# The output product of a decoder layer as one seven-product run on 512-column quarters, with loads six ahead

## The chip, the cores and the metric

The kernel runs on one core of one Trainium2 chip. The core has a matrix engine (TensorE, PE in the profile), a vector engine (VectorE, DVE), a scalar engine (ScalarE, ACT), a general engine (GpSimd, POOL) and a queue that only issues transfers (SyncE, SP). The metric is the device time of one launch in microseconds (us). The kernel before takes 770.54 us, the median of three runs (770.27 to 772.26).

## The reference

One decoder layer over 512 tokens of width 1024 in float32:

```
h = rms_norm(x, norm_mix);  proj = h @ w_in
y_pool = pool_mixer(u, w_pool);  y_nsa = nsa_mixer(q, ...)          # 16 heads, 2 groups
merged = g_a * (y_pool @ w_proj_pool) + g_b * (y_nsa @ w_proj_nsa)
x = x + merged @ w_out                                              # 512x1024 @ 1024x1024
h = rms_norm(x, norm_mlp)
x = x + square(relu(h @ w_ff1)) @ w_ff2                             # width 4096
out = rms_norm(x, norm_final)
```

`merged @ w_out` is the product that is rebuilt.

## The kernel before, in words

**Products in two halves of precision.** Each float32 operand is held as a high part H (a reduced format that PE takes at full rate) and a low part L, the rest. A product is three matmuls: H by H, H by L, L by H. A weight tile is loaded from memory (`raw`), ACT copies it to `wh` or `w3h` (the high part), and DVE subtracts to get `wl` or `w3l`. Weights that only pass through lie in three ring slots of such pairs; others have resident slots (`W1H`, `W1L` here).

**Seven products instead of eight.** A big product is cut into 2x2 blocks and computed with seven block products (Strassen's scheme in Winograd's form), named by the weight side: A11, A12, A22 are weight blocks, S1 to S4 are sums of them. The activation side has its own sums, T1 to T4. The sums of weights are not computed by an engine: SP copies one block to memory (`S<-w_ff`, `S_o<-w_out`) and POOL issues a transfer that adds the other block to it; the sum is then loaded like a weight.

**Order.** Python generators emit the instructions; each engine works through its own list in order. `pieces` and `Wide.pe` emit matmuls and, between them, call `ahead()` (which prepares the next weight) and `step_side()` (which lets each waiting side job emit its next instruction). `emit_load` issues a load when a `raw` buffer is free (there are `RAW` = 4); the table in `sums_after` says behind which load the next weight sum is begun. So a change of a product's shape moves the instructions of all engines.

**The stages around the change.** After attention come eight products pn0 to pn7 with `w_proj_nsa`, 24 matmuls of 512 columns each, which give the merged activation, 128 features at a time (`GB`, split to `mH`, `mL`). Two of the four tiles for the direct half of `w_out` are prepared between them. Then:

- columns 0 to 511 of `merged @ w_out` by seven products on quarters of 256 tokens and 256 columns (class `Out`, L1647): 168 matmuls of 256 columns, from seven weight tiles, three of which are sums made in memory and one (S4) is made by DVE from S2 and A12;
- columns 512 to 1023 directly, token tile by token tile (`tm3_resident`, L568): 96 matmuls of 512 columns from four resident tiles; after each token tile `post1` starts `to_fm(t)`.

`to_fm` is the chain that opens the MLP: add the product to x (`add_x`), sum of squares on ACT, square root, reciprocal, scale by the norm (`xs`, DVE), transposes on PE in fours (L1841), then high and low parts of the transposed activation (`R`) and the sums T1 to T4. The first products of the MLP, A11 and A12 of both column groups (`FIRST[0]`, L638), are interleaved with the chains of the last tokens; S1 of the MLP comes next and needs T1.

Of the kernel before, what the change touches and what calls it, by code (L numbers as in the profile page):

```python
# [13 lines left out]
F32 = mybir.dt.float32  # L14
FR = mybir.dt.float32r
# [47 lines left out]
def trunk(ctx: ExitStack, tc: tile.TileContext, A, out):  # L63
# [38 lines left out]
    WL, LD = [], []  # L102
    RAW = 4

# [79 lines left out]
    for j in range(8):  # L184
        add_cols(f"pn{j}", w_pn, 128 * j)
        if j in (5, 6):
            add_rows(f"wo1{j - 5}", w_o, 256 * (j - 5), 512)
    WO_LATE = {"A22": 2, "S4": 3}
    WO_TURN = ("A11", "S1", "S3", "S2", "A12", "A22", "S4")
    wo_at = {}  # L190
    late, later = [], []
    wo_of = {f"A{i + 1}{j + 1}": w_o[512 * j:512 * j + 512, 256 * i:256 * i + 256].rearrange("(k p) c -> p k c", p=128)
             for i in range(2) for j in range(2)}
    for o, x, y in (("S1", "A21", "A22"), ("S3", "A11", "A21"), ("S2", "S1", "A11")):
        wo_of[o] = dp.tile([128, 4, 256], F32, name=f"{o}_o")
        jobs.append((wo_of[o], wo_of[x], wo_of[y]))
    for o in WO_TURN:
        if o in wo_of:
            wo_at[o] = len(LD)
            LD.append([(wo_of[o], 0)])  # L200
        WL.append((f"{o}2o0", None))
        if o in WO_LATE:
            add_rows(f"wo1{WO_LATE[o]}", w_o, 256 * WO_LATE[o], 512)
    MLP0 = len(LD)
# [15 lines left out]
    def add_group(layer, c, g):  # L220

        q = quarters(layer, c, g)
        of = {"A" + k: v for k, v in q.items()}
        final = layer == 2 and c == LAST
        for o in ("S1", "S3", "S2", "S4")[:LASTSUMS if final else 4 - layer]:
            of[o] = dp.tile(list(q["11"].shape), F32, name=f"{o}_{layer}{c}{g}")
        jobs.append((of["S1"], q["21"], q["22"]))
        jobs.append((of["S3"], q["11"], q["21"]))
        if late:
            jobs.append(late.pop())  # L230
# [40 lines left out]
    raws, hls = {}, {}  # L271
    st = {"load": 0, "prep": 0, "use": 0, "kept": 0, "pairs": 0, "sums": 0}
    spare, slots_hl = [], []
# [74 lines left out]
    def shifted(tiles, key):  # L348

        o = 56 if key[-2] == "G" or key in ("ck", "ks") else 8 if key[:2] in ("wk", "wv") else 16 if key[-2] == "o" else 0  # L350
        return [t[:, o:o + 1024] for t in tiles]

    def slot_of(i):

        return shifted(slot_tiles(i), WL[i][0])
# [105 lines left out]
    def wo_steps(i):  # L461

        o = WL[i][0][:-3]
        if o in wo_at:
            while st["load"] <= wo_at[o]:
                assert emit_load()
            kept[o] = raws.pop(wo_at[o])[0]
        h, l = slot_of(i)
        t = kept.pop("A12" if o == "S4" else o)
        with behind(held_back[0]) if held_back and o == "S2" else nullcontext():  # L470
            ACT.activation(h, t, AF.Copy)
        yield
        with behind(held_back[1]) if held_back and o == "S2" else nullcontext():
            DVE.tensor_tensor(l, t, h.bitcast(F32), op=ALU.subtract)
        hls[i] = tuple(x.rearrange("p (a b) -> p a b", a=4) for x in (h, l))
        if o == "A12":
            yield
            DVE.tensor_tensor(t, t, kept["S2"], op=ALU.add)
        if o in ("A12", "S2"):
            kept[o] = t  # L480
            if o == "S2":
                return
            kept.pop("S2")
# [1091 lines left out]

    def tm3_resident(ws, aT, post):

        for t in range(NT):
            ps = bank()
            prods = []  # L1580
            for k in range(8):
                wH, wL = ws[k // 2]
                prods += split_products(*aT(k, t), wH[:, k % 2, :], wL[:, k % 2, :])
            for _ in pieces(ps, prods, prepare=t > 0):
                step_side()
            post(t, ps)

    def keep(keys, tiles):
# [12 lines left out]
    junk = [None]  # L1601

    def add_x(t, h, ps):
        DVE.tensor_tensor(X1[t][:, 512 * h:512 * h + 512], ps, X1[t][:, 512 * h:512 * h + 512], op=ALU.add)

# [124 lines left out]
    with ExitStack() as c3:  # L1730
        q3 = c3.enter_context(pool("q3"))
        gB = q3.tile([128, D], F32, name="gB1")
        nc.sync.dma_start(gB, bcast(A["norm_mlp"][0], D))
        q3.tile([128, 56], F32, name="gap")
        mT = (q3.tile([128, 8, S], FR, name="mH"), q3.tile([128, 8, S], FR, name="mL"))
        W1 = (q3.tile([128, 8, S], FR, name="W1H"), q3.tile([128, 8, S], FR, name="W1L"))
        junk[0] = q3.tile([128, 512], F32, name="junk")
        keep([f"wo1{i}" for i in range(4)], W1)

        def mTs(k, t):  # L1740
            return [m[:, k, 128 * t:128 * t + 128] for m in mT]

# [5 lines left out]
        for j in range(3):  # L1748
            split_m(j)
        w1 = []  # L1750

        class Merged:
# [42 lines left out]
        for j in range(3, 8):  # L1795
# [3 lines left out]
            fm3(f"pn{j}", post, OT)  # L1799
            if j in (5, 6):  # L1800
                w1.append(use(f"wo1{j - 5}"))
            if j >= 6:
# [8 lines left out]
        side.append(M.split())  # L1811
        first = Out("o", 0, M)
        for o in WO_TURN:
            first.pe(o)
            if o in WO_LATE:
                w1.append(use(f"wo1{WO_LATE[o]}"))

        def folded0():
            while first.done != set(first.X):
                yield  # L1820
            for n, _ in enumerate(first.fold()):
                if n % 3 == 0:
                    yield
            for t in range(NT):
                square_sum(t, 0)
            summed.append(0)
        summed = []
        side.append(folded0())

        def to_fm(t):  # L1830
            xs = q3.tile([128, D], F32, tag="xs", bufs=1, name="xs")
            add_x(t, 1, PS1[t])
            square_sum(t, 1)
            normed(t, xs)
            for _ in range(5 + (t == 0)):
                yield
            th, sl = t // 2, slice(128 * (t % 2), 128 * (t % 2) + 128)
            for a in range(2):
# [8 lines left out]
                if b != "12":  # L1847
                    DVE.tensor_tensor(XB[b][1][:, :, sl], src, XB[b][0][:, :, sl].bitcast(F32), op=ALU.subtract)
                yield
            if th == 0:  # L1850
                return
            for o, d, x, y in (("T1", XT, XQ["11"], XQ["12"]), ("T3", XQ["12"], XQ["22"], XQ["12"]),
                               ("T2", XQ["11"], XQ["22"], XT)):
                DVE.tensor_tensor(d[:, :, sl], x[:, :, sl], y[:, :, sl], op=ALU.add if o == "T2" else ALU.subtract)
                ACT.activation(XB[o][0][:, :, sl], d[:, :, sl], AF.Copy)
                yield
# [14 lines left out]

        PS1 = {}

        def post1(t, ps):
            until(lambda: summed)
            PS1[t] = ps
            g = to_fm(t)
            next(g)
            side.append(g)
        tm3_resident(w1, mTs, post1)  # L1880
    a4 = ctx.enter_context(pool("a4"))
# [70 lines left out]
    for c in range(4):  # L1952
        Y = Hidden(c == LAST)
        gs = [Group(f"1{c}{g}", XB.get, bank, (pair(GBf, 6 + g), pair(MAf, 6 + g), pair(MAf, 0), pair(MAf, 1)),
                    (lambda g, Y: lambda src, f, th: Y.act(src, g, f, th))(g, Y)) for g in range(2)]
        if c == 0:
            for o in FIRST[0]:
                for g in gs:
                    g.pe(o)
            while not turned[0]:  # L1960
# [124 lines left out]
```

## Time and profile before

| | |
|---|---|
| median of the runs | 770.54 us |
| span of the profiled execution, first to last instruction | 767.4 us |
| what lies around the span, against the median | 3.1 us |
| PE, DVE, ACT, POOL busy | 756.7, 666.4, 511.1, 184.2 us |
| granted clock of PE | full in all slices |
| pn3 to pn7 | from 378.2 |
| seven-product half of the output product | 405.4 to 425.6 |
| direct half, with the transposes | 425.6 to about 449 |
| transfers: accumulates from POOL | 50, of which 9 are issued ahead of attention, 9 in it, 32 after |

The profiled execution has no time of its own beside its span; 767.4 is the number against which its rows add up, and the median is 3.1 us above it. A busy time is the union of an engine's instructions; rows of the chain of waits give start, length and the group of instructions; rows of a window give its stretch, its length and each engine's busy time with the number of instructions.

### The profile page before, as it was taken

Reading aid. Unit: us, or ns where it says so; the run is one execution under the profiler, and the core shown is the slowest. Engines: PE = TensorE matmul, PEld = TensorE weight load, DVE = VectorE, ACT = ScalarE, POOL = GpSimd, SP = SyncE. Lnnn points to the kernel's source line nnn. Section 1 sums busy time; section 2 is a strip of 40 time slices with the busy share of each in tenths; the row PEclk is TensorE's granted clock in tenths of the full one; section 3 lists DMA queues with packets and bytes.
Section 4 is the critical chain, followed back from the end, with each engine's and each line's share of the span. In section 5 each row is a group of like instructions: output and inputs, shape, how many; then the busy total and the mean of one; then the engine's idle time right before and its main releaser. Section 6 shows DMA issues by size and latency. Waiting matters only on the chain.

```text
span 767.4 us, 13409 instructions
## 1 busy us (share of the span) xinstructions
PE 756.7 (99%) x4757; PEld 675.9 (88%) x4757; DVE 666.4 (87%) x1279; ACT 511.1 (67%) x977; POOL 184.2 (24%) x264
## 2 busy tenths in 40 slices
PE   9999999999999999999999999999999999999996
PEld 7889889888888888888889899989998999889985
DVE  7897999548988889989689689997989788978897
ACT  7766655328878888898745576954774477447754
POOL 4001010117746766574000200111111110111001
PEclk9999999999999999999999999999999999999999
DMA  9559993983051833371357965989998999799942
GB/s 308 165 143 266 251 230 108 257 214 115 15 176 52 158 56 70 56 138 60 116 186 220 324 111 185 287 219 299 310 259 222 314 303 257 215 325 294 293 171 110
DMA packets 119886, 150.76 MB, mean 196 GB/s; under 512 B 5782, under 2 KB 92346, under 8 KB 119611
## 3 DMA queue, kind: packets, MB, share of 16 engines
q1 hardware_dynamic: 98250, 122.90, 48.3%
q0 software_dynamic: 21280, 26.22, 22.8%
q8 instruction: 38, 0.62, 0.3%
q10 hardware_dynamic: 288, 0.79, 0.3%
q14 instruction: 30, 0.24, 0.1%
HBM read 145.16 MB, written 54.53 MB: 260 GB/s over the span
## 4 chain that ended last, share of the span: by engine, by line
PE 84%; DVE 9%; ACT 2%; DMA 2%; issue 1%; POOL 1%; SPq 0%; DVEq 0%; ACTq 0%; POOLq 0%
PE psB L638 20%; PE psB L1698 18%; PE psF L568 16%; PE psB L568 6%; PE psV L638 5%; PE psS L1378 4%; PE psT L1440 4%; PE psO L1474 4%; PE psB L1647 3%; DMA raw<-w_in 2%; PE psF L700 1%; DVE wl L527 1%; DVE PT L1456 1%; DVE P L1400 1%; DVE wkt L527 1%
## 5 line engine op out<-in xcount | busy, mean ns | idle before, releaser
L343 POOL DMA_DIRECT2D S<-w_ff x44 | 49.0, 1113 | 351.3 <-DMA S<-w_ff 290.3
L568 PE MATMUL psF<-R,wh 128*128 128x512 f32 x384 | 124.6, 400 | 0.0
L390 ACT ACTIVATE wh<-raw 128x1024 fp32r<-128x1024 f32 x73 | 77.1, 1058 | 70.0 <-PE psB L638 24.0
L1423 POOL TENSOR_SCALAR P<-P,sm,GT 128x128 f32<-128x128 f32 (+3 forms) x128 | 85.5, 724 | 68.8 <-DVE sm L1420 36.1
L395 DVE TENSOR_TENSOR wl<-raw,wh 128x1024 fp32r<-128x1024 f32 x73 | 88.9, 1219 | 12.7 <-ACT wh L390 12.2
L568 PEld LDWEIGHTS psF<-R,wh 128*128 128x128 f32 x384 | 68.8, 188 | 11.4 <-issue 0.2
L1410 ACT ACTIVATE P<-P,sm 128x128 f32<-128x128 f32 (+3 forms) x128 | 71.0, 557 | 9.9 <-DVE sm L1400 6.2
L568 PE MATMUL psF<-R,wl 128*128 128x512 f32 x192 | 75.5, 393 | 0.0
L524 ACT ACTIVATE wh<-raw 128x512 fp32r<-128x512 f32 (+1 forms) x76 | 45.1, 616 | 32.9 <-PE psF L568 21.2
L1400 DVE CUSTOM_DVE_ANT_0 P<-psS,cst 128x128 f32<-128x128 f32 (+3 forms) x128 | 59.3, 482 | 4.9 <-PE psT L1440 2.7
L390 ACT ACTIVATE w3h<-raw 128x1024 fp32r<-128x1024 f32 x37 | 39.2, 1059 | 34.0 <-PE psB L638 12.6
L527 DVE TENSOR_TENSOR wl<-raw,wh 128x512 fp32r<-128x512 f32 (+1 forms) x74 | 51.5, 707 | 9.2 <-ACT wh L524 8.9
L1451 ACT ACTIVATE PT<-psT 128x512 fp32r<-128x512 f32 (+2 forms) x96 | 49.0, 520 | 13.9 <-PE psT L1440 13.0
L1456 DVE TENSOR_TENSOR PT<-psT,PT 128x512 fp32r<-128x512 f32 (+2 forms) x96 | 56.2, 591 | 1.5 <-ACT PT L1451 1.3
L1440 PE MATMUL psT<-ident,P 128*128 128x128 f32 x320 | 50.1, 273 | 0.6 <-POOL rx L899 0.4
L395 DVE TENSOR_TENSOR w3l<-raw,w3h 128x1024 fp32r<-128x1024 f32 x37 | 45.1, 1220 | 4.7 <-ACT w3h L390 4.5
L1474 PE MATMUL psO<-PT,VV 128*128 128x256 f32 x320 | 48.5, 286 | 0.0
L1440 PEld LDWEIGHTS psT<-ident,P 128*128 128x128 f32 x320 | 39.6, 140 | 9.4 <-POOL rx L899 0.8
L638 PE MATMUL psB<-R,wh 128*128 128x256 f32 x336 | 46.3, 279 | 0.0
L1474 PEld LDWEIGHTS psO<-PT,VV 128*128 128x128 f32 x320 | 42.2, 188 | 1.3 <-ACT PT L1451 0.3
L638 PEld LDWEIGHTS psB<-R,wh 128*128 128x128 f32 x336 | 42.5, 188 | 0.2
L568 PEld LDWEIGHTS psF<-R,wl 128*128 128x128 f32 x192 | 36.0, 188 | 7.5
(442 smaller groups left out, 2083.7 us busy)
## 6 DMA issues: line engine op xcount, KB each, us to landing
raw<-w_ff SPq DMA_DIRECT2D x54, 512.0 KB, 6.2
S<-w_ff POOLq DMA_DIRECT2D x44, 512.0 KB, 8.2
raw<-S SPq DMA_DIRECT2D x44, 512.0 KB, 5.3
S<-w_ff SPq DMA_DIRECT2D x32, 512.0 KB, 7.3
raw<-w_in SPq DMA_DIRECT2D x31, 512.0 KB, 4.7
S<-S SPq DMA_DIRECT2D x12, 512.0 KB, 6.7
raw<-w_proj_nsa SPq DMA_DIRECT2D x8, 512.0 KB, 4.1
x<-x SPq DMA_DIRECT2D x7, 512.0 KB, 6.5
```

What stands on the lines that cost most here:

```text
L390: ACT.activation(h, t, AF.Copy)
L395: DVE.tensor_tensor(l, t, h.bitcast(F32), op=ALU.subtract)
L527: eng.tensor_tensor(l[:, sl], t[:, sl], h[:, sl].bitcast(F32), op=ALU.subtract)
L568: PE.matmul(ps, a, b, start=first and j == 0, stop=last and j == n - 1, skip_group_check=True)
L638: PE.matmul(out, w[u][:, k, 128 * f:128 * f + 128], moving[v][:, k, :], **kw)
L1400: DVE.tensor_tensor_reduce(out=P[:, o:o + n].rearrange("p (a c) -> p a c", c=128), in0=s, in1=m, scale=1.0, scalar=3e38, op0=ALU.add, op1= ...
L1410: last_exp[:] = [ACT.activation(c, c, AF.Exp, bias=sm[:, 0, e:e + 1], scale=-1.0, accum_out=sm[:, 1, e:e + 1])]
L1423: r = POOL.tensor_scalar(P[:, o:o + n], P[:, o:o + n], sm[:, 2, e:e + 1], GT[:, qb, c + e:c + e + 1], op0=ALU.mult, op1=ALU.mult)
L1440: PE.transpose(pt[:, 128 * j:128 * j + 128], P[:, 128 * j:128 * j + 128], ident)
L1456: return DVE.tensor_tensor(dL, src, dH.bitcast(F32), op=ALU.subtract)
L1474: PE.matmul(ps[:, qb % 2, :, :], VV[:, k, b, g, :], t[:, j, :, :], start=False, stop=last and j == len(kbs) - 1 and t is tL, skip_group_ch ...
L1698: PE.matmul(ps[f], self.Y.of(y)[u][:, 2 * g + k, 128 * f:128 * f + 128], w[v][:, k, :], start=first and g == k == u == v == 0, stop=g == k ...
```

## The change

The whole `merged @ w_out` becomes one seven-product run with quarters of 256 tokens and 512 columns (class `Mixed`, built on `Wide`, which the MLP's second product already uses). Each weight block of 512x512 is loaded as two halves of 256 rows: 14 halves, eight of them sums made in memory (S4 too; DVE no longer adds A12 and S2). A11, S3 and S4 go to the resident slots, the rest to the ring. The order is A11, S3, S2, A12, A22, S1, S4; S4 accumulates on the PSUM banks of S1 after S1 has been added to x, and is written out token by token so that `to_fm` of tokens 2 and 3 can follow; tokens 0 and 1 are complete after A22. The direct half is gone. The MLP's first products start when tokens 0 and 1 are shaped.

Loads run six ahead: `RAW` is 6, with two loads more at the start of the program, back to four ahead in attention (`spared`), and six again near the MLP. Sums of weights are begun earlier: POOL issues 10 accumulates ahead of attention, 16 in it and 29 after, 55 in all. `xs` has two buffers. The memory of the transfer descriptors is set to 8192 bytes instead of the default.

```diff
-    RAW = 4
+    RAW = 6
...
-    WO_TURN = ("A11", "S1", "S3", "S2", "A12", "A22", "S4")
+    WO_TURN = ("A11", "S3", "S2", "A12", "A22", "S1", "S4")
...
+    for g in range(2):
+        wo_of.append({f"A{i + 1}{j + 1}": w_o[512 * j + 256 * g:512 * j + 256 * g + 256, 512 * i:512 * i + 512].rearrange(
+            "(k p) c -> p k c", p=128) for i in range(2) for j in range(2)})
+    for o, x, y in (("S3", "A11", "A21"), ("S2", "S3", "A22"), ("S1", "A21", "A22"), ("S4", "S2", "A12")):
+        for g, of in enumerate(wo_of):
+            of[o] = dp.tile([128, 2, 512], F32, name=f"{o}_o{g}")
+            (late if o == "S4" else jobs).append((of[o], of[x], of[y]))
...
+        if i == N1 and st["spared"] < 2:
+            st["spared"] += 1
+            return True
...
+        if i == MLP0 - 6:
+            for _ in range(2):
+                emit_load()
...
-            return i in EARLY or i in (26, 27, 33, 35, 36) or N1 + 3 <= i < N1 + len(FILL2) or i == MLP0 - 2
+            return (i in EARLY or i in (26, 27, 33, 35, 36) or N1 + 3 <= i < N1 + len(FILL2) + 5) + (i in (N1 + 9, N1 + 11, N1 + 13))
         if i < MLP0 + 12:
-            return {3: 1, 6: 4}.get(i - MLP0, 0)
+            return 5 * (i == MLP0 + 6)
...
+    with behind(made[0]):
+        for _ in range(2):
+            emit_load()
...
-                for o, b, n in (("T1", "11", 1), ("T2", "22", 2), ("T4", "21", 3)):
+                for o, b, n in (("T2", "22", 1), ("T4", "21", 2), ("T1", "11", 3)):
...
-            if j in (5, 6):
-                w1.append(use(f"wo1{j - 5}"))
...
+        class Mixed(Wide):
+            def pe(self, o):
+                if o != "S4":
+                    super().pe(o)
+                    return
+                until(lambda: "S1" in self.done)
+                ws = [use(f"S42o{g}") for g in range(2)]
+                ps = self.ps["d"]
+                for f in range(2):
+                    prods = []
+                    for g in range(2):
+                        for k in range(2):
+                            y = [x[:, 2 * g + k, 128 * f:128 * f + 128] for x in self.Y.of("22")]
+                            prods += split_products(*y, *(v[:, k, :] for v in ws[g]))
+                    for _ in pieces(ps[f], prods, first=False):
+                        step_side()
+                    side.append(self.end(f, ps[f]))
+            def end(self, f, ps):
+                yield
+                x = XX[:, 2 + f, 0:512]
+                DVE.tensor_tensor(x, x, ps, op=ALU.add)
+                square_sum(2 + f, 0, 1)
+                yield from to_fm(2 + f)
...
+        mixed_o = Mixed("o", M)
+        for o in WO_TURN:
+            mixed_o.pe(o)
+        until(lambda: {0, 1} <= set(shaped))
...
+        for o in FIRST[0]:
+            for g in gs0:
+                g.pe(o)
+        until(lambda: len(shaped) == 4)
...
+    nc = bacc.Bacc("TRN2", target_bir_lowering=False, num_devices=1, dynamic_dma_scratch_size=8192)
```

Three places show how this moves instructions. The first is ACT's list in the pn stage, where the weights of pn4 to pn6 are prepared. Before (`raw_4518` is pn4's weight, `raw_4725` pn5's; `W1H` gets the tiles of the direct half):

```order
L524 ACTIVATE W1H<-raw_4828 128x512 [waits DMAHW2_49]
L524 ACTIVATE W1H<-raw_4828 128x512
L524 ACTIVATE wh_4916<-raw_4518 128x512 [waits DMAHW6_49,PE_49,Activation_49]
L524 ACTIVATE wh_4916<-raw_4518 128x512
L1746 ACTIVATE mH<-GB 128x512 [waits DVE_49]
L524 ACTIVATE W1H<-raw_4928 128x512 [waits DMAHW4_49]
L524 ACTIVATE W1H<-raw_4928 128x512
L524 ACTIVATE wh_4954<-raw_4725 128x512 [waits DMAHW7_49,PE_49,Activation_49]
L524 ACTIVATE wh_4954<-raw_4725 128x512
```

And in the change (`raw_4532` is pn4's weight, `raw_4746` pn5's, `raw_4849` pn6's; `raw_4949`, `raw_4987` are the halves of A11, `raw_5024`, `raw_5062` those of S3):

```order
L474 ACTIVATE W1H<-raw_4949 128x1024 [waits DMAHW7_49]
L519 ACTIVATE wh_4937<-raw_4532 128x512 [waits DMAHW5_49,PE_49,Activation_49]
L519 ACTIVATE wh_4937<-raw_4532 128x512
L1729 ACTIVATE mH<-GB 128x512 [waits DVE_49]
L474 ACTIVATE W1H<-raw_4987 128x1024 [waits DMAHW0_49]
L474 ACTIVATE W1H<-raw_5024 128x1024 [waits DMAHW3_49]
L519 ACTIVATE wh_4975<-raw_4746 128x512 [waits PE_49,Activation_49]
L519 ACTIVATE wh_4975<-raw_4746 128x512
L1729 ACTIVATE mH<-GB 128x512 [waits DVE_49]
L474 ACTIVATE W1H<-raw_5062 128x1024 [waits DMAHW4_49]
L519 ACTIVATE wh_5012<-raw_4849 128x512 [waits PE_49,Activation_49]
L519 ACTIVATE wh_5012<-raw_4849 128x512
```

Two tiles of output weights stood ahead of pn5's in this stretch; now three do, and the weights of pn5 and pn6 themselves no longer wait for a transfer there. A12's first half (`raw_5119`) stands ahead of pn7's in the same way.

The second place is SP's list at that time in the change; `S_210` to `S_211` are copies for sums of the MLP's weights, `S_o` are the sums of `w_out`:

```order
L339 DMA S_210_98<-w_ff 256x1x512 [waits DMAHW5_49]
L339 DMA S_111_96<-S_111_94 16x8192 [waits DMAHW6_49,DMASW0_49]
L298 DMA raw_4949<-w_out 128x2x512 [waits DMAHW7_49,DVE_49]
L298 DMA raw_4987<-w_out 128x2x512 [waits DMAHW0_49,DVE_49]
L339 DMA S_211_99<-w_ff 256x1x512 [waits DMAHW1_49]
L339 DMA S_211_100<-w_ff 256x1x512 [waits DMAHW2_49]
L298 DMA raw_5024<-S_o_73 128x1024 [waits DMAHW3_49,DVE_49]
L298 DMA raw_5062<-S_o_74 128x1024 [waits DMAHW7_49,DMAHW4_49,DVE_49]
```

Before, SP issued no such copy between pn0 and the middle of the output product; now five (with `S_210_97`) stand in the pn stage, and five accumulates on POOL belong to them and their forerunners.

The third place is DVE's list around the end of the new product, from the adds of A12's result (first row) to that of S1's first half (last row); `x` is the residual, `psB` the results, `raw_5280` an MLP weight:

```order
L1701 TENSOR_TENSOR x_4904<-x_4904,psB 128x512 [waits PE_49] x2
L477 TENSOR_TENSOR wl_5171<-raw_5178,wh_5170 128x1024 [waits DMAHW0_49,Activation_49]
L1593 TENSOR_SCALAR sq<-sq 128x1 [waits Activation_49] x2
L477 TENSOR_TENSOR W1L<-raw_5242,W1H 128x1024 [waits DMAHW2_49]
L1701 TENSOR_TENSOR x_4904<-x_4904,psB 128x512 [waits DVE_49,PE_49] x2
L399 TENSOR_TENSOR wl_5150<-raw_5280,wh_5149 128x1024 [waits DMAHW4_49,DVE_49,Activation_49]
L1600 RECIPROCAL sq<-sq 128x1 [waits Activation_49]
L1701 TENSOR_TENSOR x_4904<-x_4904,psB 128x512 [waits PE_49]
```

and PE's list at the same place:

```order
L1681 MATMUL psB<-wh_5170,R_65 128x512 x4
L563 MATMUL psB<-W1H,mH 128x512 [waits DVE_49]
L563 MATMUL psB<-W1L,mH 128x512
L563 MATMUL psB<-W1H,mL 128x512
L1849 MATMUL psB<-ident,xs 128x128 [waits DVE_49]
L1849 MATMUL psB<-ident,xs 128x128 x3
L563 MATMUL psB<-W1H,mH 128x512
```

The second row is S4's first matmul; the DVE instruction it waits for is the last of the DVE rows. Before, S1 was the second of the seven, five products ahead of S4.

More of the change, by code (lines that the diff above doesn't have):

```diff
@@ L185, in trunk @@
         add_cols(f"pn{j}", w_pn, 128 * j)
-        if j in (5, 6):
-            add_rows(f"wo1{j - 5}", w_o, 256 * (j - 5), 512)
-    WO_LATE = {"A22": 2, "S4": 3}
-    WO_TURN = ("A11", "S1", "S3", "S2", "A12", "A22", "S4")
+    WO_TURN = ("A11", "S3", "S2", "A12", "A22", "S1", "S4")
     wo_at = {}
[L191 to L196, printed above, removed]
-    for o in WO_TURN:
[L198 to L203, printed above, removed]
+    late, later, wo_of = [], [], []
+    for g in range(2):
[5 more added lines that the diff above has]
+            (late if o == "S4" else jobs).append((of[o], of[x], of[y]))
+    for o in WO_TURN:
+        for g, of in enumerate(wo_of):
+            key = f"{o}2o{g}"
+            wo_at[key] = len(LD)
+            WL.append((key, len(LD)))
+            LD.append([(of[o], 0)])
     MLP0 = len(LD)
@@ L461, in wo_steps @@
     def wo_steps(i):
[L463 to L470, printed above, removed]
+        key = WL[i][0]
+        while st["load"] <= wo_at[key]:
+            assert emit_load()
+        t = raws.pop(wo_at[key])[0]
+        h, l = dest[key][:2] if key in dest else slot_of(i)
+        late_one = held_back and key == "S22o0"
+        with behind(held_back[0]) if late_one else nullcontext():
             ACT.activation(h, t, AF.Copy)
         yield
-        with behind(held_back[1]) if held_back and o == "S2" else nullcontext():
+        with behind(held_back[1]) if late_one else nullcontext():
             DVE.tensor_tensor(l, t, h.bitcast(F32), op=ALU.subtract)
[L475 to L483, printed above, removed]
+        hls[i] = tuple(x.rearrange("p (a b) -> p a b", a=2) for x in (h, l))
         if st["load"] > RAW + MLP0:
@@ L1733, in trunk @@
         nc.sync.dma_start(gB, bcast(A["norm_mlp"][0], D))
-        q3.tile([128, 56], F32, name="gap")
+        q3.tile([128, 64], F32, name="gap")
         mT = (q3.tile([128, 8, S], FR, name="mH"), q3.tile([128, 8, S], FR, name="mL"))
-        W1 = (q3.tile([128, 8, S], FR, name="W1H"), q3.tile([128, 8, S], FR, name="W1L"))
+        W1 = [q3.tile([128, 4104], FR, name=f"W1{e}") for e in "HL"]
         junk[0] = q3.tile([128, 512], F32, name="junk")
-        keep([f"wo1{i}" for i in range(4)], W1)
-        def mTs(k, t):
-            return [m[:, k, 128 * t:128 * t + 128] for m in mT]
+        for n, o in enumerate(("A11", "S3", "S4")):
+            for g in range(2):
+                m = (2 * n + g) % 4
+                dest[f"{o}2o{g}"] = [t[:, 1024 * m + 8 * (o == "S3"):][:, 0:1024] for t in W1] + [f"W1{m}"]
         ACT.activation(tick, GB[:, 7, 0:1], AF.Sqrt)
@@ L1828, in trunk, with take @@
-        side.append(folded0())
+        class Mixed(Wide):
[8 more added lines that the diff above has]
+                    prods = []
+                    for g in range(2):
+                        for k in range(2):
[5 more added lines that the diff above has]
+            def end(self, f, ps):
+                yield
+                x = XX[:, 2 + f, 0:512]
+                DVE.tensor_tensor(x, x, ps, op=ALU.add)
+                square_sum(2 + f, 0, 1)
+                yield from to_fm(2 + f)
+            def take(self, o, ps):
+                yield from super().take(o, ps)
+                if o == "S2":
+                    for i, j in ((1, 0), (1, 1), (0, 1)):
+                        for f in range(2):
+                            x = XX[:, 2 * j + f, 512 * i:512 * i + 512]
+                            DVE.tensor_tensor(x, x, self.U[:, f, :], op=ALU.subtract if i else ALU.add)
+                            yield
+                elif o == "A12":
+                    for t in range(2):
+                        square_sum(t, 0)
+                elif o == "S1":
+                    for t in range(2, 4):
+                        square_sum(t, 1, 0)
+                elif o == "A22":
+                    for t in range(2):
+                        square_sum(t, 1)
+                    for t in range(2):
+                        yield from to_fm(t)
@@ L1854, in to_fm @@
                 DVE.tensor_tensor(d[:, :, sl], x[:, :, sl], y[:, :, sl], op=ALU.add if o == "T2" else ALU.subtract)
+                while o not in XB:
+                    yield
                 ACT.activation(XB[o][0][:, :, sl], d[:, :, sl], AF.Copy)
@@ L1870, in fourth_sum, with act0, act @@
             turned[0] += 1
[L1872 to L1880, printed above, removed]
+        shaped = []
+        mixed_o = Mixed("o", M)
+        for o in WO_TURN:
+            mixed_o.pe(o)
+        until(lambda: {0, 1} <= set(shaped))
+        Y0 = []
+        def act0(g):
+            def act(src, f, th):
+                while not Y0 or not turned[0]:
+                    yield
+                yield from Y0[0].act(src, g, f, th)
+            return act
+        gs0 = [Group(f"10{g}", XB.get, bank, (pair(GBf, 6 + g), pair(MAf, 6 + g), pair(MAf, 0), pair(MAf, 1)),
+                     act0(g)) for g in range(2)]
+        for o in FIRST[0]:
+            for g in gs0:
+                g.pe(o)
+        until(lambda: len(shaped) == 4)
     a4 = ctx.enter_context(pool("a4"))
```

49 lines of the change are left out of this document (9 added, 40 removed).

## The prediction

> **What bounds the kernel now.** First the page: which engine is busy, and what the chain that ended last is made of.
>
> ```profile
> span 767.4 us, 13409 instructions
> PE 756.7 (99%) x4757; PEld 675.9 (88%) x4757; DVE 666.4 (87%) x1279; ACT 511.1 (67%) x977; POOL 184.2 (24%) x264
> PE 84%; DVE 9%; ACT 2%; DMA 2%; issue 1%; POOL 1%; SPq 0%; DVEq 0%; ACTq 0%; POOLq 0%
> ...
> q1 hardware_dynamic: 98250, 122.90, 48.3%
> q0 software_dynamic: 21280, 26.22, 22.8%
> ```
>
> TensorE (PE) has work 99% of the span, so a matmul less is time less, unless a wait fills its place; 10.7 us of the span are PE gaps, and that is all that better feeding of PE could ever win. The span is 767.4 us, 3.1 below the median of the runs (770.54); I make the sum against 767.4 and add 3.1 at the end. A change within 0.3% (2.3 us: 768.2 to 772.9) is what a measurement of this kernel cannot tell from none.
>
> Next the chain of waits around the output product, in order of time (start, length, what).
>
> ```profile
> 378.23 27.21 PE psB L568 x120
> 405.44 20.12 PE psB L1647 x168
> 425.56 13.65 PE psB L568 x60
> 439.20 0.44 PE psB L1841 x4
> 439.64 1.39 PE psB L568 x6
> ...
> 455.27 10.74 PE psB L638 x92
> ```
>
> From 378.23 on the chain is PE alone, with no gap. The 120 matmuls are pn3 to pn7 (24 each, 0.2268 us apart): they start at 378.23, 383.67, 389.11, 394.55 and 400.0. At 405.44 begins the seven-product half of the output product (168 matmuls of 256 columns, 0.1198 each), at 425.56 the direct half (60+36 of 512 columns, 0.2275 each), between whose later pieces stand the transposes of the normed tokens in fours.
>
> Third, how full the other engines are there (span of the window, its length, busy time of PE, PEld, DVE, ACT, POOL, then clock, DMA share, GB/s).
>
> ```profile
> 360.00:380.00 20.00, 20.00 (x104) 17.01 (x103) 13.27 (x26) 15.04 (x27) 1.10 (x1) 1.00 0.39 132
> 380.00:400.00 20.00, 20.00 (x90) 16.57 (x89) 16.62 (x26) 8.13 (x14) 0.00 (x0) 1.00 0.51 159
> 400.00:420.00 20.00, 20.00 (x148) 18.96 (x148) 19.63 (x25) 12.83 (x16) 1.18 (x1) 1.00 0.79 239
> 420.00:440.00 20.00, 20.00 (x113) 17.41 (x113) 14.42 (x25) 9.48 (x20) 3.36 (x3) 1.00 1.02 329
> 440.00:460.00 20.00, 20.00 (x141) 18.41 (x140) 15.40 (x25) 14.34 (x28) 2.19 (x2) 1.00 0.71 116
> ```
>
> VectorE (DVE) is nearly full from 400 to 420 and has 10 us free from 420 to 460. The clock is full throughout.
>
> **Matmuls removed.** 168×0.1198 and 96×0.2275 are 20.12+21.84 = 41.96 us; now 168 matmuls of 512 columns run, 168×0.2270 = 38.13. The same number and width take this in the MLP:
>
> ```profile
> 567.70 38.13 PE psB L1698 x168
> ```
>
> That is **−3.83 us**, if PE never waits. Transposes and the MLP's products only change places on PE.
>
> **The wait at S4.** S1 and S4 now stand next to each other and share a PSUM accumulator, so S4's first matmul waits until DVE has added S1's result to x. Whether DVE is there in time follows from its queue. The spacing of its instructions:
>
> ```profile
> 405.67 0.68 DVE L1245 TENSOR_TENSOR GB<-psB,GB 128x512 f32<-128x512 f32 x1
> ...
> 410.24 0.68 DVE L1771 TENSOR_TENSOR R<-GB,R 128x512 fp32r<-128x512 f32 x1
> 410.85 0.69 DVE L1779 TENSOR_TENSOR GB<-GB 128x512 f32<-128x512 f32 x1
> 411.45 1.22 DVE L474 TENSOR_TENSOR wl<-raw,wh 128x1024 fp32r<-128x1024 f32 x1
> 412.58 2.35 DVE L1791 TENSOR_TENSOR R<-GB,R 128x1024 fp32r<-128x1024 f32 x2
> ```
>
> A 128x512 one follows after 0.60, a 128x1024 one after 1.13. In the changed order 7 of the first and 6 of the second kind stand from pn7's PSUM read (405.67) to the first add of a product: 4.2+6.8 = 11.0, so that add starts at 416.7, although A11 is ready at 405.4+5.45 = 410.9. With the other add DVE is through at 417.9. Then the preparation of A12's second half waits for its ring slot, which S2's first half leaves at 405.4+13.6 = 419.0; ACT needs 1.06 (below), so DVE starts at 420.1. From there to A22's first add stand seven weight lows and ten adds: 7×1.13+10×0.60+0.2 = 14.1, so 434.2; A22 was ready at 432.7. Behind that add follow, each waiting for the one before:
>
> ```profile
> L390 ACT ACTIVATE wh<-raw 128x1024 fp32r<-128x1024 f32 x5 | 5.3, 1060 | 1.4 <-PE psB L1647 1.3
> L1608 ACT ACTIVATE junk<-x 128x512 f32<-128x512 f32 x8 | 5.1, 632 | 9.1 <-DVE x L1604 6.4 <-DVE x L1673 2.5
> L1608 ACT ACTIVATION_READ_ACCUMULATOR junk<-x 128x1 f32 x8 | 1.5, 186 | 0.0
> ```
>
> the add (0.68), a square on ACT (0.63+0.19), the MLP weight's high part (1.06), its low part on DVE (1.13), a reciprocal (0.15) and then S1's add (0.68): 434.2+4.4 = 438.6, and with semaphores about 438.9. PE ended S1 at 438.1. The least wait is S1's own: its first PSUM half ends 0.45 before the product, a matmul drains in about 0.4, the add takes 0.68, so 0.6 even with DVE free (0.4 where the drain is shorter). The most: each of three ring slots that DVE waits for costs it up to a whole low, +2, so 3. **+1.5** taken: 0.8 by the count, and part of one such wait.
>
> **Behind S4.** DVE has 3 weight lows' worth more in this stage than before, and x/U additions in full width, while PE has 3.8 us less; of the 10 us free above, 3.8 go with PE's time and about 5 (2 on weights, 3 on adds) into work. The token chains (reciprocal, two scalings at 0.71, transposes, halves of T) therefore queue behind weight lows: the MLP's first product waits for R's low half behind one 1.13 low, about 0.6, and the transposes of tokens 2 and 3 up to 0.4 each. **+1.0** (0 to 2). What covers these chains is no longer the direct product but the 96 MLP matmuls of 256 columns (11.4 us) of FIRST; the chain of tokens 2 and 3 needs about that, so MLP's S1 isn't the next one late.
>
> **Earlier loads in the pn stage.** ACT's queue now holds the high parts of five output weights ahead of pn4 to pn7's, so an output weight that lands late holds up pn weights. The rows before:
>
> ```profile
> 381.84 0.37 SPq L297 DMA_DIRECT2D raw<-w_proj_nsa  x1
> ...
> 382.98 1.15 ACT L524 ACTIVATE W1H<-raw 128x512 fp32r<-128x512 f32 x2 [1.11 <-DMA raw<-w_out]
> 384.04 1.14 ACT L524 ACTIVATE wh<-raw 128x512 fp32r<-128x512 f32 x2
> ```
>
> Here pn5 is prepared at 384.04, 5.1 us before PE needs it (389.11), although ACT had waited 1.11 for an output weight. In the new order S3's first half (a sum, read back) is loaded at about the same moment as that SP row, 381.4 to 381.9, when a buffer comes free, and pn5 stands behind it: 1.06 for it, 0.62 for pn5's first high half, 0.68 for the low half, 2.36 in all. It must land by 386.75, 4.9 to 5.3 us after issue. The same holds for A12's first half ahead of pn7 (issued near 391, wanted by 397.6: 6.6 us). What a load takes:
>
> ```profile
> raw<-w_out SPq DMA_DIRECT2D x6, 512.0 KB, 4.0
> ...
> raw<-w_ff SPq DMA_DIRECT2D x4, 512.0 KB, 5.9
> S<-w_ff SPq DMA_DIRECT2D x4, 512.0 KB, 7.8
> S<-w_ff POOLq DMA_DIRECT2D x6, 512.0 KB, 10.7
> ```
>
> The first is from 370 to 410, the others from 406 to 442, where the DMA share is 1.02. Which applies? q0 carries the 50 accumulates: 22.8% of 767.4 is 175 us, 3.5 each on all 16 engines; q1 moves 122.90 MB in 371 us, 1.58 per 0.52 MB. From 360 to 406 the windows hold about 7.8+10.2+5 = 23 us of transfers; the change moves five sum copies (SP) and five accumulates (POOL) into it, +25: 48 us in 46, as full as 420 to 440. So 5.9 rather than 4.0, and pn5 0.6 to 1.0 late, at 4.0 not at all. **+0.5** (0 to 2.9, the copies' 7.8).
>
> [...]
>
> **Front.** Two extra loads at the start and six buffers can at best remove what waits for loads there:
>
> ```profile
> PE psC L997 <- DVE wkt L527: 0.7, 1, 0.7
> ...
> ACT wpl L524 <- DMA raw<-w_pool: 3.2, 1, 3.2
> ```
>
> PE waits 0.7 once; ACT's 3.2 for w_pool lies ahead of it. **−0.4** (−0.9 to 0).
>
> **Attention.** Seven more accumulates are issued there, each holding POOL 1.11 us:
>
> ```profile
> L343 POOL DMA_DIRECT2D S<-w_ff x44 | 49.0, 1113 | 351.3 <-DMA S<-w_ff 290.3
> ...
> 300.00:320.00 20.00, 19.56 (x132) 17.10 (x131) 18.84 (x60) 16.94 (x47) 12.43 (x20) 1.00 0.10 27
> 320.00:340.00 20.00, 20.00 (x133) 17.89 (x133) 17.77 (x61) 16.99 (x46) 15.64 (x24) 1.00 0.70 112
> ```
>
> Behind them in POOL's queue stand the P scalings that the transposes wait for. But the window with several accumulates (15.64 busy) has PE no less busy than the one without (12.43). **0** (0 to 2: of 7.8 us the quarter that might fall into a head's chain).
>
> **Sum.** −3.83+1.5+1.0+0.5−0.4 = −1.2: span 766.2, time **769.3**. The five extra accumulates, nine more SP rows, the smaller descriptor scratch and the wider xs lie beside PE work: POOL is 24% busy.
>
> **Rivals.** (a) DVE keeps up: S1's add waits only its 0.6, the tokens cost 0.4, the loads land at 4.0 to 5: −3.83+0.6+0.4−0.4 = −3.2, time 767.3. For it: 10 us free on DVE; against: the first add is 5.8 late already. 0.33. (b) Slower: the loads in the pn stage. It decides from a landing of about 9 us: with S3's half landing like an accumulate (10.7), pn5 is 5.6 late instead of 0.5, and everything behind shifts: 769.3+5.1 = 774.4. For it: 48 us of transfers in 46, and the scarcity of slack (5.1 us); against: SP's loads landed at 5.9 in a window as full. 0.16. (c) Attention pays: a POOL issue ahead of a P scaling delays PE by half of its 1.11: 7 of them +3.9, time 773.2. For it: POOL's queue is in order; against: the two windows above. 0.06. (d) The change doesn't take effect, since the waits eat 3.8 whole and the rest is neutral: 770.5, part of the forecast's case.
>
> **Chances.** The forecast's case with (d), 768 to 772.5: 0.41. Faster by over 0.3%: (a) and the low tail of the forecast, 0.35; within: 0.41; slower: (b), (c) and the high tail, 0.24. The range goes from 765.9 (−3.83+0.6 with all of the front's 0.9 and 0.5 more) to 774.8, past (b); the likeliest case's own is 768 to 772.
>
> **What would show it.** Right: 168 matmuls of 512 columns in about 38 us, a PE wait of 1 to 2 us on DVE's x at S4's first matmul, waits under 1 us at the transposes, pn5 starting within 1 us of pn4's end, no wait in attention that wasn't there. Wrong: no wait at S4 (then a); a wait of ACT on a load ahead of pn5 with PE idle for several us (b); more PE idle between 180 and 360 (c); or a front that is shorter by more than 0.9, from waits on loads that these views don't show.

## The result, and the profile after

The changed kernel takes **778.59 us** (median of four runs, 777.34 to 779.64) against 770.40 of the kernel before beside it: a ratio of **1.0105**, 95% interval 1.0088 to 1.0122. It is slower by 8 us, outside the predicted range of 765.9 to 774.8. The profiled execution has a span of 777.7 us (its own time 779.50), 10.3 more than before; about 2 us of these 10.3 are the spread of single executions, since the medians differ by 8.2.

The page of the changed kernel:

```profile
span 777.7 us, 13245 instructions
PE 758.9 (98%) x4661; PEld 671.3 (86%) x4661; DVE 670.8 (86%) x1282; ACT 513.1 (66%) x977; POOL 190.0 (24%) x269
PE 77%; DVE 11%; DMA 5%; ACT 3%; issue 2%; POOL 1%; SPq 0%; DVEq 0%; ACTq 0%; POOLq 0%
```

PE has 96 instructions less and still 2 us more busy time, and the chain that ended last now has 5% of DMA in it. Where, the chain of waits of the changed kernel shows in order of time (start, length, what):

```profile
378.64 5.45 PE psB L563 x24
384.09 0.62 ACT wh L519
...
386.06 4.33 DMA raw<-S_o
...
391.37 0.62 ACT wh L519
...
395.07 10.00 DMA raw<-w_out
...
405.09 1.06 ACT w3h L474
406.18 1.22 DVE w3l L477
...
408.66 7.82 PE psB L563 x22
```

Before, 120 matmuls stood here from 378.23 to 405.44 without a gap. Now pn3's 24 do (378.64), and then the chain leaves PE: an output weight is loaded (10.00 us from issue to landing), ACT makes its high part, and only then comes pn7's weight, which stands behind it in ACT's list; pn7 goes on at 408.66. PE's first matmul of the output product is at 416.30 instead of 405.28. From there the times run side by side: 82.9 us to the MLP's first output product (84.8 before) and 278.5 from there to the end (277.3 before). The loss is **10.6 us between pn3's start and the output product's**; the front and attention are 0.4 longer.

What ACT and PE waited for, from 370 to 416 for ACT, over the whole execution for PE (us in all, times, longest):

```profile
ACT W1H L474 <- DMA raw<-w_out: 7.0, 2, 6.8
ACT w3h L474 <- DMA raw<-w_out: 6.4, 1, 6.4
ACT W1H L474 <- DMA raw<-S_o: 3.3, 1, 3.3
```

```profile
PE psB L563 <- ACT wh L519: 5.2, 3, 3.3
PE psB L563 <- DVE wl L522: 1.1, 1, 1.1
...
PE psB L563 <- DVE x L1701: 0.6, 1, 0.6
PE psB L1681 <- DVE wl L399: 0.5, 1, 0.5
```

ACT stood for 16.7 us before output weights; in the kernel before, this row is all of that kind from 370 to 406:

```profile
ACT W1H L524 <- DMA raw<-w_out: 2.5, 2, 1.4
```

PE waited four times for pn4's, pn5's and pn7's weights. The wait of S4's first matmul for DVE's add of S1 is there too (`x L1701`), with 0.6. And the windows of the changed kernel (columns as in the prediction):

```profile
395.00:400.00 5.00, 5.00 (x24) 4.14 (x23) 4.27 (x7) 0.66 (x2) 0.00 (x0) 1.00 1.07 293
400.00:405.00 5.00, 3.46 (x16) 2.53 (x14) 0.00 (x0) 0.00 (x0) 0.00 (x0) 1.00 1.06 342
405.00:410.00 5.00, 2.17 (x5) 1.45 (x6) 3.82 (x6) 2.73 (x4) 0.00 (x0) 0.72 0.79 306
410.00:415.00 5.00, 5.00 (x15) 3.87 (x15) 4.80 (x8) 1.26 (x2) 0.00 (x0) 0.60 0.40 134
415.00:420.00 5.00, 5.00 (x24) 4.06 (x23) 3.65 (x6) 1.70 (x2) 0.00 (x0) 1.00 0.00 0
```

The DMA engines are full up to 405 (their share in windows of 5 us is 0.87 to 1.13 from 370 on), and DVE and ACT do nothing from 400 to 405. After the wait there is a second loss that no wait shows: the granted clock is 0.72 and 0.60, and 15 matmuls run in five us instead of 22. Matmul for matmul, the waits make 7.1 us (0.84, 1.43, 3.43, 1.37 from start to start, that is, by how much two matmuls begin further apart than the usual 0.227), the first matmuls behind the waits, 0.33 to 0.39 us apart instead of 0.227 while the clock is still 1.00, another 0.9, and the slow clock 2.6.

What fills the DMA engines, in SP's issues (start, length) and the landings of what was issued from 366 to 400 (last number: median us from issue to landing):

```profile
360.83 1.59 SPq L298 DMA_DIRECT2D raw<-S  x1
362.46 0.58 SPq L339 DMA_DIRECT2D S<-w_ff  x1
...
363.74 0.56 SPq L339 DMA_DIRECT2D S<-w_ff  x1
364.39 0.57 SPq L339 DMA_DIRECT2D S<-S  x1
373.93 2.79 SPq L298 DMA_DIRECT2D raw<-w_out  x2
376.77 1.34 SPq L339 DMA_DIRECT2D S<-w_ff  x2
```

```profile
S<-w_ff POOLq DMA_DIRECT2D x5, 512.0 KB, 10.6
raw<-w_out SPq DMA_DIRECT2D x4, 512.0 KB, 9.7
raw<-S_o SPq DMA_DIRECT2D x4, 512.0 KB, 5.9
```

In the kernel before, what was issued from 366 to 400 landed so:

```profile
raw<-w_out SPq DMA_DIRECT2D x4, 512.0 KB, 3.8
raw<-S_o SPq DMA_DIRECT2D x3, 512.0 KB, 3.3
```

Three of the five copies come right behind the load at 360.83, the other two (376.77) behind the first two output weights. The load at 360.83 is the seventh of the MLP, and it fills an extra `raw` buffer that is free from the start, so it is issued long ahead of its neighbours. The line `return 5 * (i == MLP0 + 6)` ties five sums to it. With four loads ahead the extra buffer was filled by the fifth MLP load, and the seventh, with its four sums, came after 425 us; with six ahead the same index means another moment.

### The profile page after: what moved, and what is told of

The parts are those of the page before. It is cut to its first block, busy times and chain, and to the rows that moved or that the text cites. A ratio compares the mean times of both kernels' runs of the same rounds, so it can differ in the third digit from the quotient of the medians.

```text
span 777.7 us, 13245 instructions
## 1 busy us (share of the span) xinstructions
PE 758.9 (98%) x4661; PEld 671.3 (86%) x4661; DVE 670.8 (86%) x1282; ACT 513.1 (66%) x977; POOL 190.0 (24%) x269
## 4 chain that ended last, share of the span: by engine, by line
PE 77%; DVE 11%; DMA 5%; ACT 3%; issue 2%; POOL 1%; SPq 0%; DVEq 0%; ACTq 0%; POOLq 0%
PE psF L563 18%; PE psB L633 18%; PE psB L1681 17%; PE psV L633 5%; PE psS L1376 4%; PE psO L1472 4%; PE psT L1438 4%; PE psB L563 2%; PE psF L695 2%; DMA raw<-w_out 1%; DMA raw<-S_o 1%; DMA raw<-w_pool 1%; DVE P L1398 1%; PE psC L995 1%; DVE wl L399 1%
## 5 line engine op out<-in xcount | busy, mean ns | idle before, releaser
L1421 POOL TENSOR_SCALAR P<-P,sm,GT 128x128 f32<-128x128 f32 (+3 forms) x128 | 89.2, 791 | 50.2 <-DVE sm L1418 25.8
L633 PE MATMUL psB<-R,wh 128*128 128x256 f32 x352 | 48.8, 280 | 0.0
L633 PEld LDWEIGHTS psB<-R,wh 128*128 128x128 f32 x352 | 44.5, 188 | 0.2
```

What stands on the lines that cost most here:

```text
L633: PE.matmul(out, w[u][:, k, 128 * f:128 * f + 128], moving[v][:, k, :], **kw)
L1421: r = POOL.tensor_scalar(P[:, o:o + n], P[:, o:o + n], sm[:, 2, e:e + 1], GT[:, qb, c + e:c + e + 1], op0=ALU.mult, op1=ALU.mult)
```

## The experiments

Each ratio is to the kernel before on the same chip.

**1. The five sums behind the eighth MLP load.**

```diff
-            return 5 * (i == MLP0 + 6)
+            return 5 * (i == MLP0 + 7)
...
-        while i == MLP0 + 6 and len(begun) > 2:
+        while i == MLP0 + 7 and len(begun) > 2:
```

> The changed kernel, with the five sums that it ties to the seventh MLP load tied to the eighth instead; nothing else. The seventh MLP load is the one that fills the extra buffer, which is free from the start, so it is issued at 360.83 us and the five copies and their accumulates follow it into the pn stage. Theory A (these five sums fill the DMA engines, the output weights land 9 to 10 us after issue instead of 4 to 6, and ACT's list holds pn4, pn5 and pn7's weights behind them): the copies move behind 420 us, output weights land within 6 us, the time from pn3's first matmul to the first of the output product goes from 37.8 back to 27.2 to 28.5 us, and the median from 778.6 to 767.5 to 769.5. Rival B (the order on ACT alone, three output tiles ahead of pn5, is too tight whatever the DMA engines do): pn stage still 3 us or more late, 772 or above. Rival C (the loads are late because a buffer comes free late): raw loads are issued as late as now, time within 2 us of 778.6.

Measured: 768.46 us, ratio 0.9972 (0.9961 to 0.9982). From pn3's first matmul to the output product's it takes 27.20 us, as before. What was issued from 366 to 400 now lands so:

```profile
raw<-w_out SPq DMA_DIRECT2D x5, 512.0 KB, 4.3
raw<-S_o SPq DMA_DIRECT2D x4, 512.0 KB, 4.5
```

One index takes back all of the loss. Repeated beside experiments 8 and 9 this kernel had 768.31 us, ratio 0.9988 (0.9975 to 1.0002): it is faster than before by 0.1 to 0.3%, which the first comparison tells from no change and the repetition does not.

**2. The same mistake in the kernel before.**

```diff
-            return {3: 1, 6: 4}.get(i - MLP0, 0)
+            return {3: 1, 4: 4}.get(i - MLP0, 0)
...
-        while i == MLP0 + 6 and len(begun) > 2:
+        while i == MLP0 + 4 and len(begun) > 2:
```

> The kernel before, with its four sums of the seventh MLP load tied to the fifth, which there is the one that fills the extra buffer. Theory A: three to four copies and their accumulates run in the pn stage; the two output tiles ahead of pn4 and pn5 land 7 to 10 us after issue and hold up pn weights by 2 to 6 us in all; median 772.5 to 777. Rival B (only the new order of ACT's list is at fault): pn stage stays at 27.2 us, median 770 to 771.

Measured: 776.80 us, ratio 1.0081 (1.0061 to 1.0102). Its first output weight is issued at 373.68 and lands 9.8 us later, pn4 waits for its high and then its low part (0.9 and 0.7 by the view of waits, 2.2 us with the slower matmuls behind them), and pn3 to the output product takes 29.4 us instead of 27.2. So the sums make the pn stage late without the new order of ACT's list; but only 2.2 of the 6.5 us by which its span is longer are lost there. Another 4.2 lie between 407 and 497, in waits for `wl` and `xs`; what makes those late in this kernel I did not separate.

**3. Output weights behind the pn weights on ACT, the sums left where the change has them.**

```diff
-        with behind(held_back[0]) if late_one else nullcontext():
+        with behind(held_back[0]) if late_one else behind(conv[0]):
             ACT.activation(h, t, AF.Copy)
```

> The changed kernel, with the high part of every output weight kept behind the last pn weight's on ACT; loads, copies and accumulates as in the change. Theory A: the DMA share stays near 1 and output weights still land 9 us or more after issue, but pn4 to pn7 don't wait: pn stage 27.2 to 28.5 us; the first output weights are wanted at 405, which the loads just reach, with 0 to 4 us of PE wait in the output product; median 768 to 773. Theory A would be wrong if the pn stage stayed above 33 us (then full DMA engines slow PE or the activations themselves): median 776 or above.

Measured: 772.23 us, ratio 1.0017 (1.0006 to 1.0029). The loads are as late as in the change (an output weight takes 10.0 us), and the pn stage takes 27.20 us all the same. So the price in that stage comes from the list that is worked in order: with nothing behind them there, late loads cost nothing there. The time is still 3.8 us above experiment 1, and in the profiles all of that lies between the output product's start and the MLP's first output product: DVE now has these weights' low parts in the output product, S4 waits 2.0, and behind that wait the clock falls (0.66 from 440 to 445, last section). How the 3.8 divide was not separated.

```profile
PE psB L563 <- DVE x L1701: 2.0, 1, 2.0
```

**4. Copies without accumulates.**

```diff
+        if 26 <= n <= 30:
+            return
         with tc.issue_after(behind.ins) if behind else nullcontext():
             POOL.dma_start(to, q, accum_op=ALU.add)
```

> The changed kernel without the five accumulates of the sums that are copied in the pn stage; the copies stay. (Five weight sums thus lack their second block, so the later products get other weights; the work on the engines is the same.) If the accumulates carry the load (3.5 us of all DMA engines each against 1.6 for a copy): output weights land after 5 to 7 us, pn stage 28 to 31 us, time 768 to 772. If the copies alone do it (they stand ahead of the loads on SP's own queue): output weights still land at 8 to 10 us, pn stage above 34 us, time 775 to 778.

Measured: 768.61 us, ratio 0.9968 (0.9952 to 0.9985). The copies are issued as in the change, and yet:

```profile
raw<-w_out SPq DMA_DIRECT2D x6, 512.0 KB, 4.4
raw<-S_o SPq DMA_DIRECT2D x4, 512.0 KB, 5.2
...
S<-w_ff SPq DMA_DIRECT2D x2, 512.0 KB, 5.8
```

So it is not the copies ahead of the loads on SP's queue; it is the five accumulates from POOL that are in flight while the loads are (369 to 404 us in the change). With them an output weight takes 9.7 us, without them 4.4. Two things stay open. Only two of the copies are in flight together with output weights here (the other three had landed by 373.1, before the first was issued), so the copies are tested at that number. And whether an accumulate is dear because it adds or because POOL starts it, no run separates.

**5. High priority for one weight of the MLP's first output product, on top of experiment 1.**

```diff
-        first_wide = key[:4] == "A112" and key[-1] == "1"
+        first_wide = key[:4] == "A112" and key[-1] == "1" or key == "S1200"
```

> The first experiment (sums tied to the eighth MLP load) with one more edit: the low part of the weight S1 of the MLP's first output product gets the high priority on DVE that A11's second half already has. In that experiment PE waits 0.5 to 0.7 us for it at 494 us, which neither the kernel before nor the rest of the MLP shows. Theory: the gain of the output product runs into DVE there, and 0.5 us more is kept: ratio to before 0.9960 to 0.9970. Rival: DVE is full around 484 to 498, so the wait only moves to another instruction: ratio as before that edit, 0.9972.

Measured: 768.21 us, ratio 0.9978 (0.9961 to 0.9994). The time alone cannot tell the two cases apart, since they lie 0.5 us from each other and the interval is 2.5 us wide. The trace can: the wait at 494 is gone and one for an x addition stands at 510 (0.4 us from start to start), and from the first output product of the MLP to the end it takes 278.5 us as in experiment 1.

```profile
PE psB L1681 <- DVE x L1701: 0.2, 1, 0.2
```

That is what the rival said: a wait that is pushed away comes back elsewhere.

**6. S1 early, on top of experiment 1.**

```diff
-    WO_TURN = ("A11", "S3", "S2", "A12", "A22", "S1", "S4")
+    WO_TURN = ("A11", "S1", "S3", "S2", "A12", "A22", "S4")
```

> The first experiment with the order A11, S1, S3, S2, A12, A22, S4, so that S1's result has been read long before S4 begins. Theory (S4's wait is that for DVE's addition of S1): the wait of 0.7 to 0.9 us at S4 is gone, ratio about 0.9962. Rival (the order given by the change buys cover for tokens 0 and 1, whose chain now has 5.4 us of S4 instead of 10.9 of S1 and S4): PE waits 2 to 5 us at the MLP's first products, ratio 0.999 to 1.003.

(In this order the squares of tokens 2 and 3 are summed before their last products are added, so these tokens get another norm; the work is the same.) Measured: 770.38 us, ratio 0.9987 (0.9977 to 0.9998). S4's wait is gone, and more comes in its place:

```profile
PE psB L1849 <- DVE xs L1610: 2.1, 2, 1.5
...
PE psB L633 <- DVE R L1856: 0.8, 1, 0.8
```

**7. A wait of PE by itself, in the kernel before.** ACT repeats one high half of pn7's weight.

```diff
+                for _ in range(13 if WL[i][0] == "pn7" and part["half"] == 0 else 1):
                     conv[0] = ACT.activation(h[:, sl], t[:, sl], AF.Copy)
```

> The kernel before, in which ACT makes the first high half of pn7's weight 13 times over instead of once, so that PE has to wait for it by 1 to 2.5 us. If a wait of PE costs its own length only: granted clock 1.00 after it, matmuls 0.227 us apart, the span longer by the wait.

and with 20 instead of 13:

> The same with 20 times over: PE waits 5 to 6.5 us. If the clock falls after a wait of this length, as in the changed kernel (0.60 to 0.72 from 405 to 415, matmuls 0.43 apart): 10 to 16 matmuls at 0.35 to 0.45 us, 2 to 3.5 us more than the wait itself. If that fall had another cause there: clock 1.00, the wait alone.

Measured: 779.51 and 784.65 us, one run each. The waits came out longer than I aimed at, 5.9 and 10.6. Windows of the first:

```profile
400.00:405.00 5.00, 2.54 (x12) 1.76 (x10) 4.17 (x6) 4.87 (x9) 0.00 (x0) 1.00 0.61 204
405.00:410.00 5.00, 1.51 (x4) 1.19 (x5) 2.23 (x3) 3.31 (x6) 0.00 (x0) 0.50 0.27 111
410.00:415.00 5.00, 5.00 (x20) 4.06 (x19) 1.14 (x3) 1.69 (x2) 0.00 (x0) 0.82 0.92 326
```

The clock is 0.50 from 405 to 410, and the matmuls behind the wait are 0.43 us apart instead of 0.227, for 3.1 us after the wait of 5.9 and for 6 after that of 10.6; that adds 1.8 and 3.0 us. Their edit touches no load and no sum, and the clock falls all the same: 0.50 in a window of 5 us here, 0.72 and 0.60 in those of the change.

**8. Own PSUM banks for S4, on top of experiment 1.**

```diff
-                ps = self.ps["d"]
+                ps = [bank() for _ in range(2)]
...
-                    for _ in pieces(ps[f], prods, first=False):
+                    for _ in pieces(ps[f], prods):
...
+                    for f in range(2):
+                        x = XX[:, 2 + f, 0:512]
+                        DVE.tensor_tensor(x, x, ps[f], op=ALU.add)
```

> The first experiment with PSUM banks of its own for S4, so that its first matmul need not wait until DVE has added S1; instead DVE adds S1 a second time, to the block that S4 also goes to (two adds of 128x512 more, 1.2 us of DVE). Theory (S4's wait is the shared accumulator and nothing else): the wait of 0.7 to 0.9 us at S4 goes, the two adds cost nothing on PE: 0.5 us less than the first experiment. Rival (DVE sets this stage; the wait moves to the token chains): PE waits as much or up to 2 us more at the transposes or at R's low half, time equal to the first experiment's or up to 2 us above it.

Measured: 773.16 us, ratio 1.0041 (1.0029 to 1.0053), 4.9 us above experiment 1 beside it. S4 no longer waits for S1, but the list of PE now has the transposes of tokens 0 and 1 ahead of S4, and they wait for `xs`:

```profile
PE psB L1852 <- DVE xs L1610: 4.3, 2, 3.0
```

That is more than the rival's 2 us. 1.2 us more work on DVE and another order make the waits about 3.3 us longer than in experiment 1; most of the rest is the clock, which falls behind the wait of 3.0:

```profile
440.00:445.00 5.00, 2.00 (x12) 1.52 (x11) 5.00 (x9) 3.06 (x8) 0.00 (x0) 0.91 0.72 243
445.00:450.00 5.00, 5.00 (x20) 4.03 (x19) 3.92 (x8) 2.17 (x4) 1.07 (x1) 0.75 0.96 338
```

Whether the work or the order weighs more was not separated.

**9. The front with loads four ahead, on top of experiment 1.**

```diff
-        if i == N1 and st["spared"] < 2:
-            st["spared"] += 1
-            return True
...
-    with behind(made[0]):
-        for _ in range(2):
-            emit_load()
```

> The first experiment without the two extra loads at the start of the program and without the two skipped ones before attention: loads run four ahead up to the MLP, in six buffers. Theory (the front is not bound by loads, only one PE wait of 0.7 us is): attention begins within 0.5 us of 174, time 0 to 0.7 us above the first experiment. Rival (loads six ahead give the front 1 us or more): 1 to 2 us above it.

Measured: 769.01 us, ratio 0.9993 (0.9980 to 1.0006), 0.7 us above experiment 1 beside it, with intervals that overlap.

Experiment 1 once more, on the same chip as 8 and 9:

> The first experiment once more, beside the two above on the same chip, as what they are compared with: 767.8 to 769.2 us, ratio to before 0.996 to 0.998.

## Why the prediction was wrong, step by step

**The step that failed is the size of "Earlier loads in the pn stage".** I took +0.5 and gave it an upper end of 2.9; it was +10.6. The mechanism was described there, and as rival (b): the sums moved into the pn stage, the engines full, the output weights late, the pn weights behind them on ACT. I gave it 0.16. The mis-sized number is the landing time. I took 5.9 us from loads between 406 and 442, because the DMA share is as high there. But a full share is not one thing: those loads were issued from 419.6 to 425.1 and had landed by 430.5, while the accumulates of that window, but for one (413.6 to 420.1), were issued from 432 on. So the 5.9 against 4.0, which I read as accumulates in the loads' way, stands for loads beside other loads and copies, with one accumulate at their start. In the change five of the six output weights issued with accumulates in flight took 9.2 to 10.5 us (the sixth, at 388.93, 7.0); two of S3 issued at 386.06 and 387.80, between two groups of accumulates, took 4.3 and 4.8. Experiment 4 shows that it is the accumulates and not the share: without them the share from 380 to 400 is still 0.93 (1.01 in the change), and the output weights from `w_out` land after 4.4, those from the sums after 5.2.

**What I counted only once.** I let one late load cost one wait, at pn5. The chain shows three: pn4 0.84, pn5 1.43 and pn7 3.43 and 1.37. A late load also delays the next issue, since buffers come free later: S3's first half was issued at 386.06 and not at 381.4 to 381.9 (380.42 in experiment 1). So pn5 was late although that half itself landed in 4.3 us, and the longest wait stands at pn7, behind A12's first half, which I had given 6.6 us, enough for 5.9: it was issued at 395.07 and took 10.0. And I had no term for the clock, 2.6 us, nor for the first matmuls behind a wait, 0.9.

**Where these sums came from** I took from the order alone. That one index decides whether they lie at 360 or after 420 is shown by experiments 1 and 2.

**S4's wait**: +1.5 forecast, 0.8 of it from the count of DVE's list; measured 0.6 in the change and 0.7 in experiment 1 by the view of waits (0.75 and 0.9 from start to start). The count was right: in experiment 1, where the output product starts 0.5 us later, the first add starts at 417.31 (416.7 forecast) and S1's is done at 439.5 (438.6 to 438.9 forecast; its terms add up to 0.1 more than the 4.4 given, and the 0.3 for semaphores was an estimate that no row shows: in the change's chain of waits an engine starts 0.02 us after the one it waited for, at 384.71, 416.48 and 417.20). What did not come is the part of a wait for a ring slot that I put on top.

**Behind S4**: +1.0 forecast, with 2 as its upper end; about 2.3 in experiment 1. The waits seen are small (0.2 for `R`, 0.1 at one group of transposes), but the gain of 3.8 us of matmuls, less S4's 0.9, came out as 1.8 and not 2.9 at the start of the MLP's first output product, and 1.2 more were lost after it, where PE waits for a weight's low part at 494. Experiments 5, 6 and 8 agree with DVE setting this stretch. The prediction follows DVE only as far as 460, and there its 10 free us end; in the kernel before it is nearly full from 460 to 520 (its busy time is the third of each row):

```profile
460.00:480.00 20.00, 20.00 (x174) 20.00 (x173) 19.90 (x23) 13.28 (x19) 0.00 (x0) 1.00 0.57 181
480.00:500.00 20.00, 20.00 (x133) 18.30 (x132) 18.97 (x26) 18.09 (x29) 3.24 (x3) 1.00 1.01 293
500.00:520.00 20.00, 20.00 (x90) 16.57 (x89) 20.00 (x26) 9.00 (x12) 1.15 (x1) 1.00 0.87 218
```

With the sums out of the way the forecast would have been 768.8 (−3.83+1.5+1.0−0.4); 768.3 to 768.5 were measured. That it comes so near is in part luck: S4's wait was taken 0.6 too long and what follows it 1.3 too short.

**Front**: −0.4 forecast; experiment 9 leaves it at 0 to −0.7. In the profiles attention begins at 172.98 to 174.25 in the eight with loads six ahead, and at 173.79 to 176.46 in the five with loads four ahead (173.95 before), which fits the forecast's size, but the spread of single executions is larger than that. **Attention**: 0 forecast, and the stage from there to pn3 is 0.6 us longer in the change (204.72 against 204.12): the seven accumulates cost at most that.

**How unequal the transfers are.** In experiment 4, with the copies alone, an output weight took 4.4 us (4.3 in experiment 1 without either); with the five accumulates it took 9.7. So in these runs the accumulates that POOL starts hold up the loads that SP starts, by 5.3 us between the medians. By what mechanism was not shown.

## What to carry to other kernels

When a schedule is tied to the index of a load, a change of the number of buffers can change the time at which that index happens (here from after 425 us to 360.83); look at where the tied transfers are issued before and after. For the price of a load under contention, take the row in which the same kind of transfer is in flight (9.7 us here), not one with the same DMA share (5.9). And in a list that is worked in order, as ACT's is here, one late load was a wait of whatever stood behind it: with output weights landing after 9.7 and 10.0 us, pn3 to the output product took 37.7 us in the change and 27.20 in experiment 3. Put first what is wanted first.

## What the runs showed of the hardware that I had not expected

A wait of PE cost more than its length in some of these runs, by 1.8 and 3.0 us in the two of experiment 7. After waits of 0.84 and 1.43 us in the change the granted clock stayed at 1.00, and in experiment 6, with one of 1.5, it is 0.998 over the whole execution, as in the kernel before. In experiment 3, after 2.0, the window from 440 to 445 has a clock of 0.66:

```profile
440.00:445.00 5.00, 3.91 (x14) 3.30 (x15) 4.64 (x9) 4.02 (x8) 0.00 (x0) 0.66 0.45 137
```

After 3.43 and 1.37 in the change it was 0.60 from 410 to 415, and after 5.9 and 10.6 in experiment 7 it was 0.50. In windows cut where the clock changes, the stretch at 0.50 is 3.4 us long in experiments 3 and 8, 6.8 in the change (407.20 to 414.03) and in the first run of experiment 7, and 13.7 in its second: one, two and four times the same length. The change's stretch:

```profile
407.20:414.03 6.83, 5.73 (x15) 4.22 (x14) 6.73 (x12) 1.46 (x3) 0.00 (x0) 0.50 0.55 191
```

It does not begin with the wait: in the first run of experiment 7 it begins 2.4 us after PE fell idle, in the change 0.5 us after pn7's first wait had ended.

At 0.50 the matmuls of 512 columns are 0.43 us apart instead of 0.227. This went on for 5.4 us behind the last wait in the change (408.66 to 414.03), and for 3.1 and 6 in the two runs of experiment 7. Of the waits named here the shortest with a fall behind it was 2.0 us, the longest without one 1.5. Why the clock falls, and what sets the length of the stretch, no run shows.

What is called full rate ahead of the prediction is this in the trace of the kernel before, at a granted clock of 1.00: transposes of 128 columns start 0.077 us apart (median) in the reduced format (L1348) and 0.11 in float32 (L1841), and the 512-column products of high and low parts 0.227.
